# A hybrid attention block on one core: re-ordering the work around the projection tiles of its first stage

## The chip, the cores and the metric

The kernel runs on one core of a Trainium2 chip. The metric is the device time of one execution in microseconds, the median of three runs. Engines are named as in the profile: PE is TensorE (matrix products; PEld its weight loads), DVE is VectorE, ACT is ScalarE, POOL is GpSimd, SP is SyncE, which issues the DMA transfers.

## What is computed

One layer of a diffusion backbone over 2048 latent tokens and 256 context tokens of width 1024. An adaptive norm (gain and shift from `c_act @ ada_w`) is followed by one wide projection, three mixers (pooling, differential attention, grouped-query attention), each with a SiLU gate, three branch projections with sigmoid gates, an output projection and a gated residual. Cut to what matters here:

```
shift, scale, gate = split(c_act @ ada_w + ada_b, 3)
h  = rmsnorm(x, norm_g) * (1 + scale) + shift              # and the same for the context tokens
p  = split(h @ w_in)                                       # 11 pieces, 7424 columns
dq, dk, gq, gk = rope2d(rmsnorm(piece.reshape(heads, 64), g))   # per head of 64
dv, gv         = plain pieces
diff_o = rmsnorm((softmax(q1 k1) - lam * softmax(q2 k2)) @ dv)
gqa_o  = softmax(gq gk) @ gv
y   = g0 * (b0 @ w_branch[0]) + g1 * (b1 @ w_branch[1]) + g2 * (b2 @ w_branch[2])
out = x + gate * (y @ w_out)
```

## The kernel before

Numbers that need float32 accuracy are kept as two float16 parts, high and low, and a product is three passes (high x high, high x low, low x high). There are three stages.

**First stage: norm and the attention projections.** The opening makes gain and shift from `ada_w` (`ada_product`, L219), norms the first three tiles of 128 tokens (`xnorm`), turns them on PE into `tpx` (`turned_raw`, L288) and writes the two parts into `hC` (context) and `hT` (latent): `hscaled` for the first four of the eight blocks of 128 channels, `hsecond` for the last four. In `hsecond` ACT writes the high part straight from `tpx` (L323) and DVE computes the same once more into `hf` (L325) and subtracts (L328). The weights of the first kind of projection are sized and split by `w_prepare("dv")`, a generator that the opening advances step by step.

Then `project` (L532) runs over five kinds of columns in the order dv, dk, dq, gq, gkv: for each kind 18 tiles of tokens (16 for dq and gq, which leave the context out). A tile is 24 products of 128x512 (128x256 in gkv) into a buffer `qkv`, of which there are three. Between the blocks of a tile the generators in `beside` are advanced: for dv the turning and splitting of the next three token tiles (`hmake`) and the norm of the three after (`xnorm`), for the others the preparation of the next kind's weights (`w_prepare`) and a scan of all gate columns for their largest value (`scan`: a load `scan` of 512 KB a step and an ACT pass `junk`, L447, that reads it one tile later).

A tile of dk, dq, gq and gkv is followed by a chain of four steps, `qk_chain`. Step 1: ACT squares `sq` (L362), DVE sums `s` (L364, L365), POOL the power `r` (L368) and the rope tables `ab` (L374). Step 2: DVE `nt` = `qkv` * `r` (L378), POOL `rt` = `nt` * `ab` (L382), DVE `m` (L386). Step 3: DVE the add `rt<-rt,m` (L391). Step 4: PE turns `rt` into `tpq` (L396), ACT and DVE split it into `sp` (L398, L399), SP stores `sp` to `kD` or `qD` (L402). `project` advances the chains of the older tiles by one step each, the newest first, and then runs step 1 of its own tile; so three chains are under way. In dv and gkv the values go out through `vt` and `vmax` (`v_chain`, L407, L408).

In gq (`gating`) the 16 blocks of the residual gate's columns of `ada_w` are loaded (`aw`), two in a tile, and multiplied one tile later; `ada_rows` copies the two sums to `adarow`, which shares its two buffers with the gate units' `gt`.

**Gates.** 160 gate units (40 columns of 128 by four chunks of 512 tokens; `gate_unit`, 24 products, L178) are handed out as filler: `run_gates(n)` runs n units, a unit's copy `gt` is issued with the step after its 24th. `col_split` splits the next column's weights (POOL multiplies, ACT or POOL casts, POOL subtracts). One unit stands at the end of the first stage, ahead of the last steps of the chains and the turning of `adarow` (`ada_turn`, L233); two (`HEAD_UNITS - 1`) at the head of the second.

**Second stage: attention**, 256 rows of scores (L811), softmax and the products with the values (L916, L942); the gate units are spread over it by a planner that knows how much product time is left. **Third stage:** the last twelve units, branches and output.

All engines, SP too, run their instructions in the order in which the program text issues them (`manual_schedule`); what sets the order is thus the place of a call.

## Time and profile before

| what | value |
| --- | --- |
| runs (median of 3) | 2946.96 us (2945.95 to 2947.38) |
| the profiled execution, its time | 2947.69 us |
| its span, first to last instruction | 2945.9 us |
| busy in the span: PE / DVE / ACT / POOL | 2792.9 / 2268.9 / 1623.4 / 723.1 us |
| granted PE clock, mean | 0.984 |
| first stage, to the first scores | 0 to 608 us |
| attention | 608 to about 2410 us |

The rows further down are from this one execution. A timeline row gives the start in us from the span's start, the duration, the engine (SPq: an issue by SP), the line, the operation, what it writes and reads, the count of merged instructions, and in brackets how long the engine sat idle before and what ended that. A granted clock of 1.00 is 2.4 GHz, of 0.50 1.2 GHz.

### The profile page before, as it was taken

The numbers are of one execution on the slowest core, as the hardware profiler recorded it, in microseconds if no ns is written. First come the engines' busy times: TensorE is split into PE (matmuls) and PEld (weight loads), VectorE is DVE, ScalarE is ACT, GpSimd is POOL, SyncE is SP. The second block draws the span as 40 slices with busy tenths as digits, with TensorE's granted clock in tenths as the row PEclk, the third lists the DMA queues.
The fourth block names the chain that finished last, engine by engine and source line by source line (L and its number), as shares of the span: only waits on it lengthen the run. The fifth ranks groups of instructions, "written<-read, shape, count | busy, mean of one in ns | idle before, by whom it ended". The sixth has DMA issues, their size and how long they took to land. (4 is left out here: it accounts for less than half of the span.)

```text
span 2945.9 us, 41046 instructions
## 1 busy us (share of the span) xinstructions
PE 2792.9 (95%) x15031; PEld 1651.4 (56%) x15031; DVE 2268.9 (77%) x2837; ACT 1623.4 (55%) x2168; POOL 723.1 (25%) x691
## 2 busy tenths in 40 slices
PE   6999889889999999999999999999999997999999
PEld 1544434645555554555555565555555555787787
DVE  4447666578888889888889888889888856766753
ACT  3844432247666666666766777766777752322221
POOL 1036555510201121211011111111111114533421
PEclk8999999999999999999999999999999998999999
DMA  6234552269798887889899899898988967767674
GB/s 249 108 113 121 146 154 67 66 156 187 153 187 170 164 187 166 175 174 179 182 192 193 179 179 186 167 205 180 187 172 173 189 136 236 243 222 260 205 250 153
DMA packets 1134266, 516.46 MB, mean 175 GB/s; under 512 B 985040, under 2 KB 1038704, under 8 KB 1134064
## 3 DMA queue, kind: packets, MB, share of 16 engines
q1 hardware_dynamic: 1134064, 513.84, 73.8%
q8 instruction: 118, 1.93, 0.3%
q14 instruction: 84, 0.69, 0.1%
HBM read 208.24 MB, written 78.97 MB: 97 GB/s over the span
## 5 line engine op out<-in xcount | busy, mean ns | idle before, releaser
L178 PE MATMUL gate<-hT,gws 128*128 128x512 f16 x3840 | 871.4, 380 | 0.0
L178 PEld LDWEIGHTS <-gws 128*128 128x128 f16 x3840 | 374.0, 98 | 420.8 <-issue 20.5
L819 ACT ACTIVATE pt<-sa,nm,escale 128x1024 f32<-128x1024 f32 x256 | 308.3, 1204 | 453.3 <-DVE nm L816 390.2
L811 PEld LDWEIGHTS <-qt 128*128 128x128 f16 x2560 | 250.2, 98 | 353.3 <-issue 69.6
L532 PE MATMUL qkv<-wt,hT 128*128 128x512 f16 (+1 forms) x1920 | 397.6, 363 | 0.0
L815 DVE TENSOR_REDUCE nm<-sb 128x1 f32<-128x1280 f32 x256 | 379.1, 1481 | 0.4 <-PE sb L811 0.4
L814 DVE TENSOR_REDUCE nm<-sa 128x1 f32<-128x1024 f32 x256 | 311.2, 1216 | 71.4 <-PE sa L811 62.1
L820 ACT ACTIVATE pt<-sb,nm,escale 128x1280 f32<-128x1280 f32 x256 | 360.3, 1408 | 0.0
L902 DVE SCALAR_TENSOR_TENSOR lo<-pt,nm,hi 128x2304 f16<-128x2304 f32 x128 | 340.3, 2659 | 6.1 <-ACT hi L897 4.7
L811 PE MATMUL sb<-kt,qt 128*128 128x512 f16 (+1 forms) x1536 | 320.6, 345 | 18.5 <-ACT pt L820 17.5
L897 ACT ACTIVATE hi<-pt,nm 128x2304 f16<-128x2304 f32 x128 | 283.3, 2213 | 92.0 <-issue 48.8
L532 PEld LDWEIGHTS <-hT 128*128 128x128 f16 x1920 | 190.1, 100 | 177.6 <-issue 10.8
L811 PE MATMUL sa<-kt,qt 128*128 128x512 f16 x1024 | 262.7, 379 | 20.9 <-ACT pt L819 20.2
L1189 PE MATMUL br<-bt,wt 128*128 128x512 f32 x1152 | 269.1, 394 | 2.3 <-DVE wt L1044 2.3
L942 PE MATMUL av<-th,vt 128*128 128x256 f16 x2304 | 263.4, 273 | 7.9 <-DMA th<-hi 5.1
L1189 PEld LDWEIGHTS br<-bt,wt 128*128 128x128 f32 x1152 | 218.0, 189 | 52.3 <-DVE wt L1044 3.5
L942 PEld LDWEIGHTS <-vt 128*128 128x128 f16 x2304 | 225.3, 98 | 36.3 <-issue 5.1
L926 POOL TENSOR_TENSOR o<-ot 128x256 f32<-128x256 f32 x32 | 22.0, 687 | 840.4 <-ACT ot L922 840.4
L163 POOL TENSOR_SCALAR gws<-gw 128x512 f16<-128x512 f32 x74 | 76.5, 1034 | 604.8 <-PE gate L178 600.9
L916 PE MATMUL av<-th,vt 128*128 128x256 f16 x1728 | 198.9, 273 | 0.0
L1221 PE MATMUL out<-y,wt 128*128 128x512 f32 x768 | 184.1, 398 | 11.6 <-DVE wt L1044 4.9
L916 PEld LDWEIGHTS <-vt 128*128 128x128 f16 x1728 | 169.1, 98 | 19.7
(208 smaller groups left out, 3207.8 us busy)
## 6 DMA issues: line engine op xcount, KB each, us to landing
tD<-gt SPq DMA_DIRECT2D x96, 256.0 KB
wr<-in_w_br SPq DMA_DIRECT2D x32, 768.0 KB
ld<-tD SPq DMA_DIRECT2D x96, 256.0 KB
scan<-in_w_gate SPq DMA_DIRECT2D x40, 512.0 KB
gw<-in_w_gate SPq DMA_DIRECT2D x80, 256.0 KB
qt<-qD SPq DMA_DIRECT2D x256, 64.0 KB
wr<-in_w_out SPq DMA_DIRECT2D x32, 512.0 KB
sgD<-gt SPq DMA_DIRECT2D x48, 256.0 KB
```

What stands on the lines that cost most here:

```text
L178: nc.tensor.matmul(ps, lhsT=w[:, b, k, :], rhs=hT[k][:, a, c * CH:(c + 1) * CH], start=(n == 0), stop=(n == 3 * KT - 1))
L532: nc.tensor.matmul(ps[:, :width], lhsT=tokens_of(t, k, a), rhs=wt[k][:, b, :width], start=(n == 0), stop=(n == 3 * KT - 1))
L811: nc.tensor.matmul(dst, lhsT=qt[:, s, o * P:(o + 1) * P], rhs=kt[:, k0:k1], start=(s == 0), stop=(s == 1))
L814: nc.vector.tensor_reduce(out=nm[:, 0:1], in_=sa, axis=AX.X, op=ALU.max, negate=True)
L815: nc.vector.tensor_reduce(out=nm[:, 1:2], in_=sb, axis=AX.X, op=ALU.max, negate=True)
L819: nc.scalar.activation(out=pt[:, :SA], in_=sa, func=AF.Exp, scale=escale[:, m:m + 1], bias=nm[:, 0:1], accum_out=nm[:, 2:3])
L820: nc.scalar.activation(out=pt[:, SA:], in_=sb, func=AF.Exp, scale=escale[:, m:m + 1], bias=nm[:, 0:1], accum_out=nm[:, 3:4])
L897: nc.scalar.activation(out=box["hi"], in_=pt, func=AF.Copy, scale=nm[:, 3:4])
L902: nc.vector.scalar_tensor_tensor(out=lo, in0=pt, scalar=nm[:, 3:4], in1=box["hi"], op0=ALU.mult, op1=ALU.subtract)
L916: nc.tensor.matmul(ps[:, :256], lhsT=vt[:, k, v, :], rhs=pts[a][:, k, :], start=(n == 0), stop=(n == 3 * NKT - 1))
L942: nc.tensor.matmul(ps[:, :256], lhsT=vt[:, k, :, :].rearrange("p a d -> p (a d)"), rhs=pts[a][:, k, :], start=(n == 0), stop=(n == 2 * NKT ...
L1189: nc.tensor.matmul(ps, lhsT=wb[:, a, 4 * br + k, :], rhs=branch_tile(c, br, k)[:, b], start=(m == 0), stop=(m == 11))
```

## The change

- `project` runs step 1 of its own tile first and then advances the older chains (`step_chains`).
- After the last tile the remaining steps of the chains are run between gate products, 16 products before each of the three rounds (`run_steps`), where one whole unit stood ahead of all; `HEAD_UNITS` is 4, of which two stand at the head of the second stage as before. So one more unit lies ahead of the attention, and one less in it.
- In gq a tile issues the products of the blocks that were loaded two tiles before, and then its loads; `ada_rows` comes one tile later.
- `col_split` scales and casts both halves before it subtracts.
- In the opening the last part of `hsecond` takes `hf` from ACT (`turned_tokens`, two operations a block) and POOL copies it to the high part; DVE only subtracts. `w_prepare` is advanced sooner. The first tile of dv has none of the turns of the next tokens beside it; the second and third have four each instead of three.

```diff
-HEAD_UNITS = 3
+HEAD_UNITS = 4
...
     def col_split(n):
...
-            for k in range(2):
-                wr = gate_raws.pop(0)
-                hi, lo = (w[:, s, 4 * k:4 * k + 4, :].rearrange("p k d -> p (k d)") for s in range(2))
+            parts = [[gate_raws.pop(0)] + [w[:, s, 4 * k:4 * k + 4, :].rearrange("p k d -> p (k d)") for s in range(2)]
+                     for k in range(2)]
+            for wr, hi, _ in parts:
                 nc.gpsimd.tensor_scalar(out=wr, in0=wr, scalar1=gws[:, 0:1], scalar2=1.0, op0=ALU.mult, op1=ALU.mult)
...
+            for wr, hi, lo in parts:
                 nc.gpsimd.tensor_tensor(out=lo, in0=wr, in1=hi, op=ALU.subtract)
...
+    def run_steps(n):
+
+        for _ in range(n):
             if next(dense, None) is None:
                 break
+
+    def run_gates(n):
+        run_steps(24 * n)
...
-                tp = turned_raw(0, k)
-                hf = sp.tile([P, GT], F32, name="hf", tag="hf", bufs=4)
-                for (a, b, m), (_, _, d) in zip(spans(0), targets(0, k, 0)):
-                    nc.scalar.activation(out=d, in_=tp[:, a:b], func=AF.Identity, scale=gainS[:, k, m:m + 1],
-                                         bias=shiftS[:, k, m:m + 1])
-                    nc.vector.tensor_scalar(out=hf[:, a:b], in0=tp[:, a:b], scalar1=gainS[:, k, m:m + 1],
-                                            scalar2=shiftS[:, k, m:m + 1], op0=ALU.mult, op1=ALU.add)
+                hf = turned_tokens(0, k, gainS, shiftS)
+                for a, b, d in targets(0, k, 0):
+                    nc.gpsimd.tensor_scalar(out=d, in0=hf[:, a:b], scalar1=1.0, scalar2=1.0, op0=ALU.mult, op1=ALU.mult)
...
-            next(c)
-            chains.append(c)
...
+            if new:
+                next(new)
+            step_chains()
+            if new:
+                chains.append(new)
+
+        def step_chains():
             for c in chains[::-1]:
                 if next(c, "end") == "end":
                     chains.remove(c)
...
-                    at_step(making, *((2, 5, 7), (1, 3, 6), (0, 2, 4))[i])
+                    at_step(making, *(((2, 5, 7), (1, 3, 6), (0, 2, 4)) if g else ((), (1, 3, 5, 7), (0, 2, 4, 6)))[i])
...
-                if gating and u < 9:
-
-                    for m in range(2 * u, 2 * u + 2):
+                if gating and u < 10:
+
+                    for m in (2 * u - 4, 2 * u - 3):
+                        if 0 <= m:
+                            ada_product(gps[m % 2], m // 2, ada_raws.pop(0))
+                    for m in (2 * u, 2 * u + 1):
                         if m < 16:
...
-                        if m >= 2:
-                            ada_product(gps[m % 2], (m - 2) // 2, ada_raws.pop(0))
-                elif gating and u == 9:
+                elif gating and u == 10:
                     rws = ada_rows(gps)
...
-        run_gates(1)
         while chains:
-            for c in list(chains):
-                if next(c, "end") == "end":
-                    chains.remove(c)
+            run_steps(16)
+            step_chains()
         gmod = ada_turn(rws)
...
-                run_gates(HEAD_UNITS - 1)
+                run_gates(HEAD_UNITS - 2)
```

On DVE, a tile of dk (the newest tile's squares are `sq_2176` before and `sq_2221` after; `qkv_2120` is the tile before it). Before:

```order
L378 TENSOR_TENSOR nt_2157<-qkv_2058,r8_2115 128x512
L386 TENSOR_TENSOR m2_2161<-nt_2157,ab_2117 128x512
L391 TENSOR_TENSOR rt_2093<-rt_2093,m2_2095 128x512
L399 TENSOR_TENSOR sp2_2169<-tpq_2164,sp2_2169 128x512
L364 TENSOR_REDUCE s8_2178<-sq_2176 128x8
L365 TENSOR_SCALAR s8_2178<-s8_2178,wedk_1484 128x8
L489 SCALAR_TENSOR_TENSOR wt_2199<-wraw_1500,wsd_2137,wt_2199 128x512
L489 SCALAR_TENSOR_TENSOR wt_2202<-wraw_1502,wsd_2137,wt_2202 128x512
L378 TENSOR_TENSOR nt_2221<-qkv_2120,r8_2181 128x512
```

After:

```order
L489 SCALAR_TENSOR_TENSOR wt_2199<-wraw_1500,wsd_2137,wt_2199 128x512
L489 SCALAR_TENSOR_TENSOR wt_2202<-wraw_1502,wsd_2137,wt_2202 128x512
L364 TENSOR_REDUCE s8_2223<-sq_2221 128x8
L365 TENSOR_SCALAR s8_2223<-s8_2223,wedk_1484 128x8
L378 TENSOR_TENSOR nt_2231<-qkv_2120,r8_2162 128x512
L386 TENSOR_TENSOR m2_2235<-nt_2231,ab_2164 128x512
L391 TENSOR_TENSOR rt_2169<-rt_2169,m2_2171 128x512
L399 TENSOR_TENSOR sp2_2243<-tpq_2238,sp2_2243 128x512
```

The two sums moved from the end of a tile's group to its head; before, the sums `s8_2178` are followed by `nt_2221`, which needs their power `r8_2181`; after, `nt_2231` needs `r8_2162`, whose sums were written a tile earlier.

On ACT, the end of the first stage and the start of the second (`sp2` are the key copies of the last chains, `gt` a gate unit's copy, `gws` a gate column's cast). Before:

```order
L161 ACTIVATE gws_5568<-gw_4929 128x512
L161 ACTIVATE gws_5568<-gw_4931 128x512
L398 ACTIVATE sp2_5606<-tpq_5604 128x128
L398 ACTIVATE sp2_5619<-tpq_5617 128x128
L398 ACTIVATE sp2_5626<-tpq_5624 128x128
L184 ACTIVATE gt_5685<-gate_5579,ginv_121 128x512
L184 ACTIVATE gt_5713<-gate_5688,ginv_121 128x512
```

After:

```order
L161 ACTIVATE gws_5568<-gw_4929 128x512
L161 ACTIVATE gws_5568<-gw_4931 128x512
L398 ACTIVATE sp2_5605<-tpq_5603 128x128
L185 ACTIVATE gt_5617<-gate_5579,ginv_121 128x512
L398 ACTIVATE sp2_5632<-tpq_5630 128x128
L398 ACTIVATE sp2_5654<-tpq_5652 128x128
L185 ACTIVATE gt_5713<-gate_5620,ginv_121 128x512
```

The copy of the first gate unit moved ahead of the last two key copies.

On POOL, the opening (`rs` belongs to the norm, `wt` are the high parts of the weights, `hC` and `hT` the high parts of the tokens). Before:

```order
L265 TENSOR_TENSOR rs_435<-ss_376,mhalf_110 128x3
L485 TENSOR_SCALAR wt_449<-wraw_217,wsd_360 128x512
L485 TENSOR_SCALAR wt_452<-wraw_219,wsd_360 128x512
L485 TENSOR_SCALAR wt_467<-wraw_221,wsd_360 128x512
L485 TENSOR_SCALAR wt_470<-wraw_223,wsd_360 128x512
```

After:

```order
L485 TENSOR_SCALAR wt_434<-wraw_217,wsd_354 128x512
L485 TENSOR_SCALAR wt_437<-wraw_219,wsd_354 128x512
L269 TENSOR_TENSOR rs_441<-ss_376,mhalf_110 128x3
L326 TENSOR_SCALAR hC_142<-hf_448 128x256
L326 TENSOR_SCALAR hT_443<-hf_448 128x128
L485 TENSOR_SCALAR wt_455<-wraw_221,wsd_354 128x512
L485 TENSOR_SCALAR wt_458<-wraw_223,wsd_354 128x512
L326 TENSOR_SCALAR hC_142<-hf_466 128x256
L326 TENSOR_SCALAR hT_461<-hf_466 128x128
```

Two weight casts moved ahead of `rs`, and the copies of the tokens' high parts were added.

## Rows read from the trace of the kernel before

**Rows 1.** Stage windows: busy us (count) of PE, PEld, DVE, ACT, POOL; clock; DMA.

```profile
0.00:608.00 608.00, 533.88 (x2639) 265.94 (x2640) 357.25 (x686) 239.24 (x503) 252.28 (x294) 0.95 0.43 127
608.00:2410.00 1802.00, 1757.17 (x10247) 996.49 (x10246) 1593.06 (x1786) 1244.01 (x1496) 279.55 (x260) 1.00 0.87 178
```

**Rows 2.** Timeline of the opening: first products, scaling of the next tokens, their turns.

```profile
58.54 3.20 PE L532 MATMUL qkv<-wt,hC 128*128 128x512 f16 x9
...
68.14 2.07 DVE L268 TENSOR_SCALAR xt<-xt,rs 128x1024 f32<-128x1024 f32 x3
...
69.04 1.04 PE L288 MATMUL tpx<-ident,xt 128*128 128x128 f32 x2 [7.30 <-DVE xt L268]
```

**Rows 3.** Timeline of PE, dk to the start of gq.

```profile
203.82 5.34 PE L532 MATMUL qkv<-wt,hT 128*128 128x512 f16 x24
...
209.44 5.34 PE L532 MATMUL qkv<-wt,hT 128*128 128x512 f16 x24
...
312.90 0.69 PE L396 MATMUL tpq<-ident,rt 128*128 128x128 f32 x4 [4.16 <-DVE rt L391]
313.38 7.01 PE L532 MATMUL qkv<-wt,hT 128*128 128x512 f16 x24
...
411.00 3.57 PE L219 MATMUL ada<-aw,cct 128*2 128x512 f32 x4 [6.56 <-DMA aw<-in_ada_w]
...
420.82 1.88 PE L219 MATMUL ada<-aw,cct 128*2 128x512 f32 x4
```

**Rows 4.** Timeline of DVE, POOL, ACT and SP, one tile of dk.

```profile
224.54 0.68 DVE L399 TENSOR_TENSOR sp<-tpq,sp 128x512 f16<-128x512 f32 x1
...
226.16 1.64 POOL L368 TENSOR_TENSOR r<-s,mhalf 128x8 f32<-128x8 f32 x1 [2.09 <-DVE s L365]
...
226.98 0.59 ACT L362 ACTIVATE sq<-qkv 128x512 f32<-128x512 f32 x1
227.19 0.47 SPq L509 DMA_DIRECT2D scan<-in_w_gate  x1
...
227.82 0.69 DVE L378 TENSOR_TENSOR nt<-qkv,r 128x512 f32<-128x512 f32 x1 [1.75 <-POOL r L368]
...
228.62 0.69 DVE L386 TENSOR_TENSOR m<-nt,ab 128x512 f32<-128x512 f32 x1
228.69 1.75 POOL L382 TENSOR_TENSOR rt<-nt,ab 128x512 f32<-128x512 f32 x1 [0.33 <-DVE nt L378]
229.23 1.75 DVE L391 TENSOR_TENSOR rt<-rt,m 128x512 f32<-128x512 f32 x1
230.91 0.68 DVE L399 TENSOR_TENSOR sp<-tpq,sp 128x512 f16<-128x512 f32 x1
231.17 1.06 ACT L447 ACTIVATE junk<-scan 128x1024 f16<-128x1024 f32 x1 [3.60 <-DMA scan<-in_w_gate]
```

**Rows 5.** Timeline: two weight operations on DVE beside the power on POOL.

```profile
251.46 1.41 DVE L489 SCALAR_TENSOR_TENSOR wt<-wraw,wsd,wt 128x512 f16<-128x512 f32 x2
251.64 2.07 POOL L368 TENSOR_TENSOR r<-s,mhalf 128x8 f32<-128x8 f32 x1 [2.09 <-DVE s L365]
```

**Rows 6.** Timeline of PE, end of gq, gkv and the end of the stage.

```profile
497.10 5.34 PE L532 MATMUL qkv<-wt,hT 128*128 128x512 f16 x24
...
567.62 0.45 PE L396 MATMUL tpq<-ident,rt 128*128 128x128 f32 x1 [3.78 <-DVE rt L391]
...
572.98 2.78 PE L532 MATMUL qkv<-wt,hT 128*128 128x256 f16 x24
...
581.44 5.34 PE L178 MATMUL gate<-hT,gws 128*128 128x512 f16 x24
...
592.55 0.47 PE L396 MATMUL tpq<-ident,rt 128*128 128x128 f32 x1 [5.65 <-DVE rt L391]
...
595.30 12.86 PE L178 MATMUL gate<-hT,gws 128*128 128x512 f16 x48
```

**Rows 7.** Timeline of SP: the first key loads of the attention.

```profile
602.15 1.24 SPq L776 DMA_DIRECT2D kt<-kD  x2
```

More of the change, by code (lines that the diff above doesn't have):

```diff
@@ L199, in block_kernel @@
     dense = gates()
-    def run_gates(n):
-        for _ in range(24 * n):
+    def run_steps(n):
+        for _ in range(n):
             if next(dense, None) is None:
                 break
+    def run_gates(n):
+        run_steps(24 * n)
     with tc.tile_pool(name="p1", bufs=1) as sp, tc.tile_pool(name="p1s", bufs=1, space=PSUM) as pp:
@@ L536, in project @@
                     next(s, None)
+            e = weps[kind]
+            new = None
+            if kind == "dk":
+                new = qk_chain(ps, 8, GAIN["dk"], t, e, lambda i: (kD[i], t))
+            elif kind == "dq":
+                new = qk_chain(ps, 8, GAIN["dq"], t, e, lambda i: (qD[i], t - NCT))
+            elif kind == "gq":
+                new = qk_chain(ps, 8, GAIN["gq"], t, e, lambda i: (qD[4 + i], t - NCT))
+            elif kind == "gkv":
+                v_chain(ps, 128, 128, gvD, 1, t)
+                new = qk_chain(ps, 2, GAIN["gk"], t, e, lambda i: (kD[4], t))
+            else:
+                v_chain(ps, 0, 512, vD, 0, t)
+            if new:
[4 more added lines that the diff above has]
+        def step_chains():
             for c in chains[::-1]:
@@ L539, in project @@
                     chains.remove(c)
-            e = weps[kind]
-            if kind == "dk":
-                c = qk_chain(ps, 8, GAIN["dk"], t, e, lambda i: (kD[i], t))
-            elif kind == "dq":
-                c = qk_chain(ps, 8, GAIN["dq"], t, e, lambda i: (qD[i], t - NCT))
-            elif kind == "gq":
-                c = qk_chain(ps, 8, GAIN["gq"], t, e, lambda i: (qD[4 + i], t - NCT))
-            elif kind == "gkv":
-                v_chain(ps, 128, 128, gvD, 1, t)
-                c = qk_chain(ps, 2, GAIN["gk"], t, e, lambda i: (kD[4], t))
-            else:
-                v_chain(ps, 0, 512, vD, 0, t)
-                return
-            next(c)
-            chains.append(c)
         xs, hf0, chains, beside = {}, [], [], {}
@@ L646, in block_kernel @@
                     next(wp)
-            if n == 14:
-                next(wp)
-            if n == 15:
+            for _ in range({13: 2, 14: 1, 15: 2}.get(n, 0)):
                 next(wp)
         rws = ada_rows(aps[1])
-        next(wp)
-        for _ in range(2):
-            next(wp)
         norming = xnorm(1)
@@ L662, in block_kernel @@
             next(hs)
+        next(wp)
         next(norming)
```

## The prediction

> **What bounds the kernel now.** I read the stage windows first. From 608 to 2410 us TensorE is busy 1757.17 of 1802 us, 97.5%; from 0 to 608 it is busy 533.88 of 608, and at a granted clock of 0.95 instead of 1.00 [rows 1]. So the attention stage is at TensorE's pace, and the first stage, which nearly all of the edits touch, has 74 us in which TensorE does nothing, and some more that it loses at the lower clock level. The chain of waits of that stage, and then the timeline, say where they lie.
>
> An unhindered tile of dk, dq or gq takes 5.62 us (203.82 to 209.44) [rows 3]. But TensorE gets there only while it has slack. In the dk tiles VectorE goes round in 6.37 us (sp2 at 224.54, again at 230.91) [rows 4]. The reader is to see one idle gap in that ring: `nt` waits 1.75 us for `r`, which POOL starts only after VectorE has written the two sums, since the sums of the newest tile stand last in VectorE's order and `nt` of the same tile comes next. The second thing to see is `rt` on POOL (1.75) beside the add `rt<-rt,m` on VectorE (1.75), against 0.69 for `m`, which has the same shape [rows 4]: the two lie on each other. When the slack is gone TensorE's turns wait for the add.
>
> **The change, part by part** (against the profiled execution, 2947.69 us; its span is 2945.9, and the median of the runs, 2946.96, is 0.7 us below it).
>
> *Sums first (B: dk, dq, start of gq).* Now VectorE does the sums of tile t, then `nt`, `m` of t-1, the add of t-2, `sp` of t-3. Nothing is added; `r` has a whole tile to arrive, so the 1.75 us wait goes. VectorE's work for a tile is 0.94 (the two sums, between 225.22 and 226.16), 0.69, 0.69, the add, and 0.68 [rows 4]. With the add at 0.69, as `m` has it, that is 3.7 us; at 1.75 it is 4.75. Both are below 5.62. What is late next is a ring through the scan of the gate columns: `sp` to the next scan issue on SP (224.54 to 227.19, 2.65, the stores lie between), issue to the `junk` that reads it (227.19 to 231.17, 3.98), `junk` 1.06, `sq` 0.59, which now stands behind `junk` and ahead of all of the chain, then 0.94 + 0.69 + 0.69 + the add until `sp` again [rows 4]. That is 11.3 us with the short add and 12.35 with the long one, for two tiles: 5.65 or 6.2 us a tile. In the new order the add runs while POOL does `r` and `ab`, not `rt`. The nearest row for such an overlap is a pair of `wt` operations beside `r`: they take 1.41 for two, and it is `r` that stretches, from 1.64 to 2.07 [rows 4, 5]. So I take the short add and 5.7 us a tile.
> From 203.82 to the end of gq's second tile (411.00 less its 6.56 us of waiting, 404.4) are 31 tiles: 200.6 us [rows 3]. At 5.7 they take 176.7: 23.9 less. One event I leave in: where the next weights' loads come in a burst, TensorE waits 4.16 us for the add and then runs a tile of 5.34 us in 7.01 [rows 3]; the burst is still there, and half of it, 3 us, may stay. **B = 21**, with ends 8 (6.2 us a tile) and 26 (5.62).
>
> *Gate columns two tiles ahead (C).* The first products of the gate rows wait 6.56 us for their load, and four of them then take 3.57 where four take 1.88 later [rows 3]: 8.2 us. The loads keep their place; the products come one tile, 5.6 us, later. So some 1 us of waiting is left. **C = 7**, ends 5 and 8.2. That ada products stand beside tiles u = 2 to 9 instead of 1 to 8 costs nothing, there are 16 in either.
>
> *The end of gq, and gkv (D).* From 497.10 to the first gate product at 581.44 are 84.3 us [rows 6]. It holds two tiles of 5.62, eighteen gkv tiles of 2.78, and beside three of these still the wide turns, 0.3 each (5.62 less 5.34): 62.2 at full pace, 22.1 less. gkv has the same ring in small, and the same wait goes. Kept: some 2 us at the entry, where three wide chains (3.7 each) meet tiles of 3 us, and 1.5 of the 3.78 us [rows 6] behind the split of the first gate column on POOL; both halves now go to ScalarE before POOL subtracts. **D = 18.5**, ends 11 and 22.
>
> *Last stages between gate products (F, G).* From 581.44 to the end of 48 gate products at 608.16 (595.30 + 12.86) TensorE takes 26.7 us for 72 products, 5.65 of it in one wait for an add, and 48 products cost 12.86 rather than 10.7 since the clock had dropped [rows 6]. The new order has 96 products there, 21.4, and three turns (0.47 at most) and the turned gate rows, all of it some 2.0 of the 2.75 between 592.55 and 595.30: 23.4. A wait is added: the copy `gt` of the first gate unit uses the buffer of the gate rows, so ScalarE waits in it until these are turned; queued behind it are the last two key copies, their stores, the value scales and the loads of the attention. Today the first keys are issued at 602.15, 6.85 us after the turned rows' end [rows 6, 7]; with `gt` and two copies ahead some 8.5. The 48 products cover 10.7, and the keys must land by then: 0 to 3 us of waiting, I take 0.5. **F = 3**, ends 0 and 5. The 24 products more are 24 fewer in the attention, at 97.5% on TensorE: 5.3 at most, **G = 4**, ends 0 and 5.3.
>
> *The opening (A).* The first tile holds three sets of turns of the next tokens, and TensorE waits 7.30 us for them, until VectorE has scaled the tokens at 68.14; nine products before it took 3.20 us, 0.36 each, where warm ones take 0.22 [rows 2, 3]. The turns leave that tile (four in each of the next two instead of three), VectorE loses eight operations on the way to the scaling, POOL gains eight, and the weights' scale is made some us sooner. No row shows POOL's copies; they stand behind weight casts on POOL, which VectorE waits for anyway. Upper end: the 7.30 and 24 products back at the full rate, 10. Lower: ScalarE, with eight turns' copies and three squares now in two tiles, gives 4 back: 3. **A = 8**, near the wait, which has no other owner.
>
> Nothing else moves: columns of the gate weights keep their POOL time, only re-sorted. Sum: 8 + 21 + 7 + 18.5 + 3 + 4 = 61.5; 2947.7 - 61.5 = 2886, and with the 0.7 us to the median **2885 us**.
>
> **Rivals.** *1. VectorE's two-operand operations lose to POOL.* In today's ring `m` starts 0.07 us before `rt`, and `rt` is long; the add starts after `rt` and is long [rows 4]: who comes first keeps the other off. If `r` (1.64) and the two `ab` keep `m` and the add off in the same way, the add costs 1.75 or more, the ring 6.2 us: B = 8, and gkv pays 0.4 in each of 15 tiles: D = 12. Sum 42: 2905. Against it: the pair of `wt`, two operands from the same memory, beside `r`, was not slowed [rows 5].
> The Trainium skill has this as a rule (SBUF — State Buffer, "Who interferes with whom"): VectorE with two SBUF inputs and a GpSimd operation that reads SBUF exclude each other for the whole instruction, the first one winning. `rt` against the add agrees with it; `wt` beside `r` does not, at least not for the whole of `r`. By the rule this rival would be the forecast.
> *2. Everything at TensorE's pace*: all upper ends, 76 us: 2870. It needs the burst and the first loads to vanish too.
> *3. The scan still sets the pace.* If its loads take a microsecond or two longer at the faster pace, a tile stays at 6.4, B is 2 and A 4: 2915 to 2930. For it: SP issues scan and stores in one order; against: ScalarE waits 3.60 us for the scan today without TensorE feeling it.
> *4. Slower.* In the new order POOL's `r`, `ab` and `rt` all fall beside `m` and the add. If both must sit out what POOL has queued, `m` waits for `r` and `ab` (about 2.3) and the add for `rt`: the two-tile ring is 14 us, 7.0 a tile, B = -16 and gkv some 9 over. That alone is the break-even with A, C, F and G. From 7.0 us a tile on it is slower; with TensorE's clock dropping in each of those gaps (7.01 for 5.34 [rows 3]) it costs some 10 us more: 2960. That needs every arbitration lost, where the rows show one lost and one won.
> That the edit is not what it says can be left out: the order on each engine shows it.
>
> **How the numbers follow.** Forecast (2872 to 2895): 0.58. Rival 1 (2895 to 2914): 0.25. Rival 2 (2866 to 2872): 0.08. Rival 3: 0.06. Rival 4: 0.03. A range of 2869 to 2914 leaves out rivals 3, 4 and half of 2. The measurement can tell 0.2% (6 us) from no change. Faster: 0.96; same 0.015, for rival 4 at its break-even; slower 0.025.
>
> **What would show it.** VectorE's `nt` no longer waits for `r`, and its add beside `r` takes about 0.7, not 1.75 (1.75: rival 1). TensorE's turns in dk and dq have no wait over 0.3 us apart from the burst; gkv tiles go every 2.7 to 2.9 us. The first ada product waits under 2 us. The first turn of the second token group comes near 65, not 69. The first scores begin some 55 us sooner than today. I am wrong if ScalarE's `sq` is found waiting behind `junk` tile after tile, or if the first scores wait for keys for more than 3 us.

## The result, and the profile after

The kernel after takes 2910.44 us (median of 4 runs, 2908.53 to 2912.96) against 2947.17 beside it: ratio 0.9878, interval 0.9866 to 0.989. It is faster by 36.7 us, at the slow end of the range (2869 to 2914), where 61.5 us were forecast. The direction and the mechanism of the largest term came out, but only F had its size: A was too low, and B, C, D and G were too high.

To see where, I take the same marks in both traces and ask how much sooner each comes. "Sooner" is the lead over the kernel before; what the lead grows from one mark to the next is what the stretch between them gave, and it stands under "measured" beside the term of the prediction for that stretch (us).

| mark | before | after | sooner | term | forecast | measured |
|---|---|---|---|---|---|---|
| dv, fourth tile | 88.34 | 77.05 | 11.30 | A opening | 8 | 11.3 |
| gq, second tile | 397.90 | 370.40 | 27.50 | B sums first | 21 | 16.2 |
| gq, eleventh tile | 473.97 | 444.88 | 29.09 | C gate rows | 7 | 1.6 |
| first gate product | 581.44 | 540.43 | 41.01 | D end of gq, gkv | 18.5 | 11.9 |
| first scores | 608.00 | 563.70 | 44.30 | F last stages | 3 | 3.3 |
| first branch product | 2468.36 | 2431.40 | 36.96 | G attention | 4 | -7.3 |
| end | 2945.88 | 2908.19 | 37.7 | | | 0.7 |

The miss, 23.8 us, is G (11.3), D (6.6), C (5.4) and B (4.8), less the 3.3 that A brought more and 1.0 in F and behind the last mark. The windows of the kernel after show both sides (columns as in [rows 1]): the first stage is 44 us shorter and still has 34 us in which TensorE is idle, and the attention, with 24 products fewer in it, is longer than before, where the same stretch took 1860.36.

```profile
0.00:563.70 563.70, 529.75 (x2663) 269.68 (x2664) 313.92 (x678) 239.87 (x504) 233.31 (x304) 0.96 0.47 138
563.70:2431.40 1867.70, 1797.84 (x10412) 1014.80 (x10413) 1621.91 (x1826) 1256.55 (x1516) 299.14 (x278) 0.99 0.87 179
```

**An unhindered tile of dk after** (timeline; it answers to [rows 4]): `nt` follows the newest sums with no wait, the add stands beside `r` and takes 0.69, and VectorE is done with the tile in 3 us. From here to the end of dk the tiles go at 5.62 us, but for two with the products of the next weights' scale in them (5.72 and 6.03) and the last, 6.40. `sq` stands behind a `junk` that waits for the scan, 4.05 us, and TensorE does not feel it.

```profile
205.01 0.68 DVE L378 TENSOR_TENSOR nt<-qkv,r 128x512 f32<-128x512 f32 x1
205.18 1.64 POOL L368 TENSOR_TENSOR r<-s,mhalf 128x8 f32<-128x8 f32 x1 [2.02 <-DVE s L365]
205.80 0.69 DVE L386 TENSOR_TENSOR m<-nt,ab 128x512 f32<-128x512 f32 x1
206.41 0.69 DVE L391 TENSOR_TENSOR rt<-rt,m 128x512 f32<-128x512 f32 x1
207.51 1.26 POOL L382 TENSOR_TENSOR rt<-nt,ab 128x512 f32<-128x512 f32 x1
209.26 1.06 ACT L447 ACTIVATE junk<-scan 128x1024 f16<-128x1024 f32 x1 [4.05 <-DMA scan<-in_w_gate]
210.32 0.58 ACT L362 ACTIVATE sq<-qkv 128x512 f32<-128x512 f32 x1
```

**Where the next weights are loaded**, TensorE now stops for longer than before. In dq (first group below) SP issues eight weight loads and behind them the scan's; ScalarE's `junk` waits 6.30 us for it, `sq` comes behind, and TensorE waits 4.92. Two tiles take 11.14 and 7.65, the second in part at the lower clock level (granted clock 0.69 from 288.3 to 296.4); [rows 3] had a wait of 4.16. In gq the same happens (second group): the gate columns' product does not wait any more, where it waited 6.56 us in [rows 3], but the turn ahead of it does.

```profile
273.04 3.79 SPq L460 DMA_DIRECT2D wraw<-in_w_qkv  x8
276.88 0.43 SPq L509 DMA_DIRECT2D scan<-in_w_gate  x1
283.58 1.06 ACT L447 ACTIVATE junk<-scan 128x1024 f16<-128x1024 f32 x1 [6.30 <-DMA scan<-in_w_gate]
288.34 1.08 PE L396 MATMUL tpq<-ident,rt 128*128 128x128 f32 x4 [4.92 <-DVE rt L391]
...
372.23 4.04 SPq L460 DMA_DIRECT2D wraw<-in_w_qkv  x8
381.74 1.06 ACT L447 ACTIVATE junk<-scan 128x1024 f16<-128x1024 f32 x1 [6.66 <-DMA scan<-in_w_gate]
386.50 1.08 PE L396 MATMUL tpq<-ident,rt 128*128 128x128 f32 x4 [4.71 <-DVE rt L391]
387.51 3.57 PE L223 MATMUL ada<-aw,cct 128*2 128x512 f32 x4
```

**gkv**: its steady tiles take 2.73 us (3.42 before). At the entry the add meets POOL's `rt` and takes 1.75, TensorE waits 3.04 and then has the lower clock for a tile (granted clock 0.54 from 488.9 to 495.2). Such a tile, at the lower clock level after a wait, is called cold from here on. Behind the first column's split ScalarE's copy waits for POOL, the next tile's `vt` and `sq` stand behind it, and TensorE waits 2.38, with a cold tile again (4.45 for 24 products that take 2.78 otherwise).

```profile
486.44 1.75 POOL L382 TENSOR_TENSOR rt<-nt,ab 128x512 f32<-128x512 f32 x1
486.98 1.75 DVE L391 TENSOR_TENSOR rt<-rt,m 128x512 f32<-128x512 f32 x1
488.88 1.09 PE L396 MATMUL tpq<-ident,rt 128*128 128x128 f32 x4 [3.04 <-DVE rt L391]
...
521.11 1.30 ACT L161 ACTIVATE gws<-gw 128x512 f16<-128x512 f32 x2 [2.87 <-POOL gw L159]
522.32 0.26 ACT L407 ACTIVATE vt<-qkv 128x128 f32<-128x128 f32 x1
524.96 0.33 PE L396 MATMUL tpq<-ident,rt 128*128 128x128 f32 x1 [2.38 <-DVE rt L391]
525.12 4.45 PE L532 MATMUL qkv<-wt,hT 128*128 128x256 f16 x24
```

**The first scores** (here `sa`) wait 0.78 us behind the gate products; the forecast had 0.5 for the keys.

```profile
552.40 10.52 PE L179 MATMUL gate<-hT,gws 128*128 128x512 f16 x48 [0.53 <-ACT gt L185]
563.70 1.02 PE L812 MATMUL sa<-kt,qt 128*128 128x512 f16 x4 [0.78 <-POOL gws L163]
```

**In the attention** one row of scores takes 13.19 us where the same row took 6.52 before. That is 6.7 us. The stage is 7.3 us longer, and 24 products fewer should have made it some 5 us shorter (0.22 us each), so nearly as much again is lost in other rows, such as the one at 670.91 (8.45, 6.52 before) and the one at 2242.88 (9.96, 8.70 before). In the long row it goes like this: POOL splits a gate column; SP stands in the load that refills the column's buffer until the subtraction is over; the transposed loads of the parts (`th`) stand behind that load on SP, which has hardly a pause from there to the one issued at 1465.36; for that one TensorE waits, three rows after the one in which the hold began, and then runs at the lower clock level (0.22 us a product, where 36 take 4.09 below).

```profile
1442.92 4.58 POOL L165 TENSOR_TENSOR gws<-gw,gws 128x512 f16<-128x512 f32 x2
1444.11 3.76 SPq L150 DMA_DIRECT2D gw<-in_w_gate  x2
1449.28 2.83 SPq L849 DMA_TRANSPOSE th<-hi  x1
1465.36 4.32 SPq L849 DMA_TRANSPOSE th<-hi  x1
1471.74 4.00 PE L943 MATMUL av<-th,vt 128*128 128x256 f16 x18 [3.34 <-DMA th<-hi]
```

Ahead of the same row of the kernel before, the load came when the subtraction was over, and the products did not wait:

```profile
1497.02 1.16 POOL L164 TENSOR_TENSOR gws<-gw,gws 128x512 f16<-128x512 f32 x1
1499.45 0.87 SPq L150 DMA_DIRECT2D gw<-in_w_gate  x2
1510.73 4.09 PE L942 MATMUL av<-th,vt 128*128 128x256 f16 x36
```

### The profile page after: what moved, and what is told of

The parts are those of the page before. It is cut to its first block, busy times and chain, and to the rows that moved or that the text cites. A ratio compares the mean times of both kernels' runs of the same rounds, so it can differ in the third digit from the quotient of the medians.

```text
span 2908.2 us, 41087 instructions
## 1 busy us (share of the span) xinstructions
PE 2787.0 (96%) x15031; PEld 1653.7 (57%) x15031; DVE 2222.6 (76%) x2829; ACT 1623.7 (56%) x2168; POOL 699.2 (24%) x699
## 5 line engine op out<-in xcount | busy, mean ns | idle before, releaser
L532 PEld LDWEIGHTS <-hT 128*128 128x128 f16 x1920 | 189.7, 99 | 176.8 <-issue 11.3
L163 POOL TENSOR_SCALAR gws<-gw 128x512 f16<-128x512 f32 x74 | 68.2, 922 | 597.7 <-PE gate L179 593.8
```

The lines of the kernel that those rows point to most:

```text
L532: nc.tensor.matmul(ps[:, :width], lhsT=tokens_of(t, k, a), rhs=wt[k][:, b, :width], start=(n == 0), stop=(n == 3 * KT - 1))
```

## The experiments

Times are medians; the kernels of one group shared the runs of the kernel before (2947.67, 2946.87 and 2947.70 us in the three groups). "First scores" and "attention" (first scores to first branch product) come from the profiled execution of each kernel. The code is cut; `...` marks what is left out.

### The sums first alone

On the kernel before, only this (the loop over the older chains becomes `step_chains`, and is called behind the new tile's first step):

```diff
+            if new:
+                next(new)
+            step_chains()
+            if new:
+                chains.append(new)
+
+        def step_chains():
             for c in chains[::-1]:
                 if next(c, "end") == "end":
                     chains.remove(c)
...
-            next(c)
-            chains.append(c)
```

> The kernel before with one part of the change alone: a tile's sums and its first step are issued ahead of the older tiles' steps (opening, gate columns, last stages as before). Theory 1 (the sum's terms B and D were too large, since the stalls where the next weights and the first gate columns are loaded, and the entry into gkv, do not go away with the order): tiles of dk and dq at 5.62 us but one tile of dq near 11 us; gained by the end of gq's second tile 14 to 18 us, over gq's end and gkv 9 to 13, attention as before (first scores to the first branch product 1860 us): about 2921 us (2915 to 2927). Theory 2 (the terms were right, B = 21 and D = 18.5, and what the sum missed was lost elsewhere by the other edits): 2947 - 39.5 = about 2908. Theory 3 (the add is slowed beside POOL, 6.2 us a tile): tiles at 6.2 us, about 2927 to 2930, with the add at 1.75 us in the rows.

Measured: 2930.12 us, ratio 0.9944 (0.9927 to 0.996): 17.5 us, a smaller gain than any theory but the third had. Theory 3 falls all the same, since the tiles of dk go at 5.62 and not at 6.2, although the total is about the one that it gave. What theory 1 has right are the stalls: a dq tile takes 12.27, the first tile with gate rows 17.04, and the split's tile 6.90. It missed one: with the products one tile behind their loads, gq has further tiles of 10.00, 9.00 and 10.86, and the lead over the kernel before falls from 13.6 us to 5.2 across them. At the first scores it is 20.9; the attention takes 1863.0.

### Gate rows one tile behind their loads

```diff
-                if gating and u < 10:
+                if gating and u < 9:
...
-                    for m in (2 * u - 4, 2 * u - 3):
+                    for m in (2 * u - 2, 2 * u - 1):
...
-                elif gating and u == 10:
+                elif gating and u == 9:
```

> The kernel after, with the products of the gate rows one tile behind their loads, as in the kernel before, in place of two. Theory 1 (the distance is worth more than the 1.6 us by which the lead grows across these tiles, since in the kernel with the sums first alone, where the products stand one tile behind, the lead fell by 8.4 us across the same tiles, with tiles of 10.00, 9.00 and 10.86 us where 7.53 is the pace): several gq tiles of 9 to 11 us, first scores 8 to 12 us later than 563.7, total 2918 to 2922. Theory 2 (the burst of loads costs the same either way and the distance gives the 1.6 to 3.5 us read from the lead): 2911 to 2914. Theory 3 (the term C = 7 of the sum): 2916 to 2918.

Measured: 2920.25 us (0.9912, 0.9897 to 0.9927), 9.8 us over the kernel after; first scores at 576.34. Theory 1 holds. The products wait for their loads at every second tile:

```profile
387.28 3.57 PE L223 MATMUL ada<-aw,cct 128*2 128x512 f32 x4 [8.03 <-DMA aw<-in_ada_w]
407.63 1.88 PE L223 MATMUL ada<-aw,cct 128*2 128x512 f32 x4 [2.82 <-DMA aw<-in_ada_w]
442.47 2.65 PE L223 MATMUL ada<-aw,cct 128*2 128x512 f32 x4 [2.79 <-DMA aw<-in_ada_w]
```

Across these tiles the lead falls from 24.4 to 14.4 us. So the distance is worth about 10 us, and the 1.6 of the table is not its worth but what is left of it after the stall in gq: with the sums first and the old distance, 8 to 10 us are lost there.

### Weight loads spread

```diff
-            if not final:
+            if n == 0:
                 for k in range(KT):
                     w_load(QKV_ORDER[n + 1], k)
...
+                if n and not final and u < 4:
+                    for k in (2 * u, 2 * u + 1):
+                        w_load(QKV_ORDER[n + 1], k)
                 project(kind, width, wt, t)
```

> The kernel after, with the eight loads of the next weights (for dk, dq and gq) issued two at a time ahead of the first four tiles, in place of eight ahead of the first. Theory 1 (the two long stalls after the change, one dq tile of 11.14 us and the gq tile of 14.57 us, are the scan's load that stands behind eight weight loads, with ScalarE's squares behind the scan): both go, the dq tiles stay at 5.62 us and the first gq tile with gate columns takes 7.5 to 8.5; first scores at 547 to 552 us instead of 563.7, total 2895 to 2899. Theory 2 (it is the bytes of that stretch, so that spreading only spreads the delay): first scores within 4 us of 563.7 and several tiles near 7 us; 2907 to 2911.

Measured: 2902.91 us (0.9848, 0.9833 to 0.9863), between the two theories; first scores at 558.81, though its opening was 2 us late. The gq tile falls from 14.57 to 8.48. In dq the stall is only drawn out: tiles of 6.31, 7.95 and 7.30 in place of 11.14 and 7.65. Two weight loads ahead of each scan are enough to make TensorE wait:

```profile
289.97 1.06 ACT L447 ACTIVATE junk<-scan 128x1024 f16<-128x1024 f32 x1 [5.22 <-DMA scan<-in_w_gate]
294.72 0.63 PE L396 MATMUL tpq<-ident,rt 128*128 128x128 f32 x4 [2.14 <-DVE rt L391]
```

### A third buffer for the scan

The burst stays, and the scan is loaded a tile earlier. The room comes from two other tiles, which lose a buffer each: `ab` has two instead of three, and `vt` of the value tiles one instead of two (these lines are left out):

```diff
...
-            for i in range(41):
+            for i in range(42):
                 if i < 40:
-                    t = sp.tile([P, D], F32, name="scan", tag="scan", bufs=2)
+                    t = sp.tile([P, D], F32, name="scan", tag="scan", bufs=3)
...
-                if i:
-                    size_of(gmx[:, i - 1:i], tiles[i - 1])
+                if i > 1:
+                    size_of(gmx[:, i - 2:i - 1], tiles[i - 2])
```

> The kernel after, with three buffers for the scan of the gate columns in place of two: each load is issued one tile earlier than it is read (room for it from one buffer less of vt in the value tiles and of ab). Theory 1 (the two-tile ring through the scan has no slack, so each burst of weight loads stops ScalarE's squares and TensorE for as long as it lasts; 2 x 256 KB ahead of each scan already cost a stall of 7.95 us and a cold tile of 7.30 in the spread version): the dq tile of 11.14 us and its cold successor go to 5.62 to 6.5, the gq tile of 14.57 to 7.5 to 9; first scores at 548 to 552 instead of 563.7; total 2894 to 2899. Theory 2 (TensorE waits for VectorE's add for another reason there, such as the weights' sizes on ScalarE behind their own loads): the stalls stay above 9 and 12 us; 2906 to 2912.

Measured: 2892.97 us (0.9816, 0.9799 to 0.9832), 17.5 us under the kernel after; first scores at 545.72. Theory 1 holds: the dq tiles take 5.62 (5.73 and 6.03 with the scale's products in them), and the gq tile 8.45. By gq's eleventh tile, with the opening set apart, 15.8 us are gained; the rest is in gkv, where this execution has one cold tile less. A scan still lands late behind the eight weight loads, but it is read a tile later, and the turn that waited 4.92 us waits no more:

```profile
273.02 3.79 SPq L460 DMA_DIRECT2D wraw<-in_w_qkv  x8
276.85 0.44 SPq L509 DMA_DIRECT2D scan<-in_w_gate  x1
283.52 0.60 PE L396 MATMUL tpq<-ident,rt 128*128 128x128 f32 x4
284.14 1.06 ACT L447 ACTIVATE junk<-scan 128x1024 f16<-128x1024 f32 x1 [4.34 <-DMA scan<-in_w_gate]
289.14 0.60 PE L396 MATMUL tpq<-ident,rt 128*128 128x128 f32 x4
```

### Three gate units ahead, as before

```diff
-HEAD_UNITS = 4
+HEAD_UNITS = 3
...
-            run_steps(16)
+            run_steps(8)
...
-                run_gates(HEAD_UNITS - 2)
+                run_gates(HEAD_UNITS - 1)
```

> The kernel after, with three gate units ahead of the scores as in the kernel before, in place of four: 8 gate products in each round of the last stages in place of 16, and 48 ahead of the second row. Theory 1 (the attention is 7 us longer after the change, 1867.7 us from the first scores to the first branch product against 1860.4, because the gate columns' splits and loads fall on other rows, above all behind the row where TensorE waits 3.3 us for a transposed load): attention back to 1859 to 1863 though it has 24 products more, first scores 2 to 5 us sooner than 563.7; total 2898 to 2905. Theory 2 (the loss comes with the earlier start, whatever the number of units): attention 1870 to 1874 with the 24 products, total 2909 to 2914.

Measured: 2901.26 us (0.9849, 0.9834 to 0.9864); attention 1862.49 with 24 products more in it, first scores at 560.97. Theory 1 holds: the row of 13.19 us takes 6.52 again. The row's stall is there in all six other kernels that have the attention of the kernel after unchanged (the list below the next heading), wherever between 545 and 577 us their first scores come. It goes with how the columns fall on the rows, not with the time of the start. The re-sorted `col_split` is in this kernel too, so it does not make the stall by itself; whether four units with the old split would have it is not shown.

### The next gate column loaded one unit later

```diff
             gate_split.append(w)
-            col_load(n + 2)
...
             gate_now[0] = gate_split.pop(0)
+        if u % NCH == 1:
+            col_load(u // NCH + 3)
...
                         col_split(0)
+                        col_load(2)
```

> The kernel after, with the load of the next gate column issued on SP one gate unit later than the split that frees its buffers, in place of right behind it. Theory 1 (in the attention SP waits in that load for POOL's last subtraction, 3.7 us between 1444.1 and 1447.9, and the transposed loads stand behind it, so TensorE waits for them some rows later): no wait of TensorE for a transposed load over 2 us, attention 1858 to 1863 us instead of 1867.7; total 2900 to 2906. Theory 2 (the transposed loads are late because the DMA engines are full, 0.91 busy in that stretch): waits of about the same sum, 1865 to 1870; total within 4 us of 2910.

Measured: 2898.07 us (0.9832, 0.9818 to 0.9847), 12.4 us under the kernel after, though its first scores come 2.5 us later; attention 1852.38, more gained than theory 1 had it. The stage is shorter with the DMA engines as full as in the kernel after (0.88 against 0.87), so theory 2 falls. SP now issues the transposed load before POOL has begun to subtract, 7 us sooner, and the one for which TensorE waited 5.4 us sooner; the products of that row do not wait. TensorE's waits for transposed loads fall from 16.7 us in all to 1.7 (7.7 in the kernel before). Besides the row of 13.19 us, which takes 6.52, three more rows gain most: 9.96, 9.47 and 8.45 us become 6.74 each.

```profile
566.16:2418.54 1852.38, 1794.30 (x10412) 1014.23 (x10412) 1620.75 (x1825) 1255.58 (x1516) 297.29 (x277) 1.00 0.88 180
```

```profile
1442.01 2.74 SPq L851 DMA_TRANSPOSE th<-hi  x1
1442.70 4.58 POOL L165 TENSOR_TENSOR gws<-gw,gws 128x512 f16<-128x512 f32 x2
1456.40 0.89 SPq L150 DMA_DIRECT2D gw<-in_w_gate  x2
1459.99 3.88 SPq L851 DMA_TRANSPOSE th<-hi  x1
1468.01 4.09 PE L945 MATMUL av<-th,vt 128*128 128x256 f16 x36
```

The attention of all kernels (us), the kernels with three units ahead first: before 1860.35, sums first alone 1863.0, three units 1862.5; four units: after 1867.7, third scan buffer 1869.1, weights spread 1868.1, gate rows near 1869.3, turns back 1865.9, split in steps 1866.7, early weights 1869.1; with the later loads 1852.4.

### The later load on the kernel before

The same edit on the kernel before:

```diff
-            col_load(n + 2)
...
+        if u % NCH == 1:
+            col_load(u // NCH + 3)
...
+                        col_load(2)
```

> The kernel before, with the load of the next gate column issued one gate unit later than the split that frees its buffers, and nothing else. With that edit the kernel after went from 1867.7 to 1852.4 us between the first scores and the first branch product. Theory 1 (the hold of SP costs the kernel before less, as its columns fall on better rows, and without it both take the same time but for the 24 products, 5.1 us): 1856 to 1859 us there instead of 1860.4, total 2942 to 2946; the term G was right but for the hold. Theory 2 (the hold costs the kernel before as much): 1847 to 1850, total 2933 to 2937. Theory 3 (no hold in the kernel before at all): 1860, total 2946 to 2948.

Measured: 2943.80 us (0.9989, 0.998 to 0.9998), attention 1858.42. Theory 1 holds. Without the hold of SP the kernel before takes 1858.4 and the kernel after 1852.4; the 6.0 us between them are about what the 24 products take (5.3). Kernels with one and the same attention differ by up to 3.4 us in the list above, so no more is read from that, and the 1.9 us by which the attention got shorter here is not clear of it; the 3.1 us of the total are clear of noise. SP's waits in that load during the attention are, of the kernel before and of the kernel after (us in total, times, longest):

```profile
SPq L150 <- POOL gws L164: 43.6, 22, 4.4
```

```profile
SPq L150 <- POOL gws L165: 47.5, 24, 3.6
```

The hold is nearly as large in both. Without it the attention gets 1.9 us shorter in the one and 15.3 in the other: what it costs depends on the rows on which it falls. The difference, 13.4 us, covers the 11.3 by which G missed.

### The turns back in the first tile

```diff
-                    at_step(making, *(((2, 5, 7), (1, 3, 6), (0, 2, 4)) if g else ((), (1, 3, 5, 7), (0, 2, 4, 6)))[i])
+                    at_step(making, *((2, 5, 7), (1, 3, 6), (0, 2, 4))[i])
```

> The kernel after, with the turns of the second token group in all three first tiles (three, three, two), as in the kernel before, in place of the last two; the earlier weight steps and POOL's copies in the opening stay. Theory 1 (the 11.3 us of the opening are the wait of 7.3 us for the turns and the clock behind it): a wait of 5 to 8 us in the first tile is back, first scores 8 to 10 us later than 563.7. Theory 2 (the earlier scaling of the tokens and the shorter way of VectorE make most of it): the wait is under 3 us, first scores 0 to 4 us later.

Measured once: 2910.97 us. The wait is back, 5.20 us and cold products behind it, and the fourth tile comes 6.2 us later; the other edits of the opening thus bring 5.1 of the 11.3, and which of them is not told apart. The rows are the first tile here and then in the kernel after:

```profile
56.17 3.22 PE L532 MATMUL qkv<-wt,hC 128*128 128x512 f16 x9
64.59 1.05 PE L292 MATMUL tpx<-ident,xt 128*128 128x128 f32 x2 [5.20 <-DVE xt L272]
```

```profile
55.87 9.28 PE L532 MATMUL qkv<-wt,hC 128*128 128x512 f16 x30
64.98 0.38 PE L292 MATMUL tpx<-ident,xt 128*128 128x128 f32 x2
```

At gq's eleventh tile it is 7.8 us behind the kernel after, at the first scores only 2.7, and in the total nothing. So the wait is theory 1's, and the first scores are theory 2's. In gkv this execution did not have the cold tiles behind the waits (2.78 where the kernel after had 5.20, and again 2.78 for 4.45), and the attention was 1.9 us shorter. One run does not say whether that repeats.

### The first column's split in steps, and the gkv weights earlier

The first spreads the split over the gkv tiles 8 to 14 (POOL scaling with its copy, again, a subtraction, again; the generator `col_split_steps` is left out); the second takes four steps of the weights more in gq:

```diff
-                    if u == 10:
-                        col_split(0)
+                    if u == 8:
+                        splitting = col_split_steps(0)
+                    if u in (8, 9, 11, 13, 14):
+                        next(splitting, None)
...
```

```diff
                         at_step(coming, 3)
+                    if gating and u in (10, 11, 12, 13):
+                        at_step(coming, 5)
```

> The kernel after, with the split of the first gate column in five steps over the gkv tiles 8 to 14 (one POOL scaling with its ScalarE copy, then the other, then one subtraction, then the other) in place of all of it behind tile 10. Theory 1 (TensorE's wait of 2.38 us there and the slow tile behind it come from the 5.1 us that POOL spends in one piece ahead of the next tile's r): no wait over 0.6 us in those tiles, first scores 2.5 to 4.3 us sooner than 563.7 for an equal opening. Theory 2 (a subtraction of 1.15 us beside 1.8 us of a tile's own POOL work is more than the 2.73 us of a tile has room for): two waits of 0.3 to 1 us, 1 to 2 us sooner.

> The kernel after, with four more steps of the gkv weights' preparation in gq's tiles 10 to 13, so that the last casts and VectorE's small operations on the scale are done some tiles before gkv begins. Theory 1 (VectorE's 1.84 us of casts and 1.55 us of small operations, which stand in the last gq tile and the first gkv tile, are why the entry into gkv loses 3.97 us in its second tile and 1.2 in its first): the first two gkv tiles take 2.8 to 4.5 us each instead of 3.95 and 6.70, first scores 3 to 6 us sooner for an equal opening. Theory 2 (it is the wide chains of gq's last tiles, with the add of 1.75 us behind POOL's rt): the second tile stays at 5.5 to 6.7, under 1.5 us sooner.

Measured once each: 2908.05 and 2908.82 us. In the first, neither theory has the cause. TensorE waits twice, 1.39 and 1.54 us, behind the two scalings and not behind the subtractions: ScalarE's copy stands at the head of its queue until POOL has scaled, and the next tile's `vt` and `sq` stand behind it. The two tiles lose 3.4 us where the kernel after lost 4.3.

```profile
515.05 0.63 ACT L159 ACTIVATE gws<-gw 128x512 f16<-128x512 f32 x1 [2.88 <-POOL gw L158]
515.58 0.26 ACT L420 ACTIVATE vt<-qkv 128x128 f32<-128x128 f32 x1
517.90 0.33 PE L409 MATMUL tpq<-ident,rt 128*128 128x128 f32 x1 [1.39 <-DVE rt L404]
```

In the second, the second gkv tile takes 4.77 in place of 6.70, and the wait is 1.53 in place of 3.04: half of that tile's loss was the casts and the scale's small operations on VectorE, as theory 1 has it; the other half stays, with the add of 1.75 us, as theory 2 has it. The first tile keeps its 3.95.

### Together

The third scan buffer with the later column loads:

> The kernel after with two edits that were run apart, the third scan buffer (2893.0) and the later gate column loads (2898.1). Theory 1 (they lie in different stages and add): 2910.4 - 17.5 - 12.4 = 2880.5 (2876 to 2884), attention near 1852 us, first scores near 547. Theory 2 (how the attention's columns fall changes with the start, so that its gain is in part luck): attention 1857 to 1866, 2885 to 2892.

Measured: 2878.88 us (0.9768, 0.9755 to 0.9781), first scores at 549.59, attention 1853.26. Theory 1 holds: the two add.

And with the split in steps and the early weights besides:

> The kernel with the third scan buffer and the later gate column loads, and also the split of the first gate column in five steps and the earlier gkv weights. Expected from the theories of the four: 2880.5 less 2.6 for the split and 3 to 5 for the entry, 2872 to 2877. If the last two edits do nothing, 2880; if POOL's subtractions or the added steps disturb the gkv and gq tiles, above 2882.

Measured: 2877.23 us (0.9759, 0.9746 to 0.9773), at the upper edge of what was expected and not told apart from the one without them. By its median it is the fastest of the kernels, some 33 us under the kernel after and 70 under the kernel before. Its first scores come at 546.62, and its attention takes 1852.28.

## Why the prediction was right or wrong

**B, the mechanism: right; the size: not.** `nt`'s wait went and the tiles reached TensorE's pace, a little better than the 5.7 us that I took. The step that failed is "half of it, 3 us, may stay", for the burst. The stall there grew to 7.6 us (11.14 and 7.65 less two of 5.62). I had the ring through the scan at 11.3 us for two tiles, which is right, and then used it as a rate. With TensorE at 11.24 for two tiles that ring has no slack, and so a late load passes whole into TensorE's time. That is rival 3 in small: the scan does not set the pace, it sets the stalls. The third buffer shows it. The term of 3 us for the burst thus measured 7.6, and that is nearly all of the 4.8 us by which B missed.

**C: the wrong owner.** The step that failed is "some 1 us of waiting is left". The product's own wait did go, but the same burst delays the scan, and the turn ahead of the product waits 4.71 us. It was also mis-sized the other way: at the new pace the old distance would have cost some 10 us more than I knew of, as the kernel with it shows. The two roughly cancel.

**D: two kept terms mis-sized.** For the entry into gkv I kept 2 us; its first three tiles lost 7.9 (3.95, 6.70 and 5.47 less 2.73 each), of which I had counted 0.9 as wide turns; half of the wait there comes from casts and small operations that I had not looked for in that tile. For the column's split I kept 1.5; it took 4.3, and its cause is not POOL's subtraction, which the re-sorting moves, but ScalarE's copy that waits at the head of its queue. Some of both is the lower clock behind the wait. The steady tiles were right (2.73, forecast 2.7 to 2.9).

**F: right** (3.3, forecast 3): behind the 48 products the first scores wait 0.78 us, where I took 0.5.

**G: right as work, wrong as time.** The two kernels without the hold are 6.0 us apart there, where I had 5.3 at most for the 24 products. The step that failed is that I counted them as a pure loss of work in a stage at 97.5%. One unit more ahead of the stage also shifts the gate columns against the rows of scores, and in the kernel after one column's load holds SP's queue just where the transposed loads are wanted. I listed SP among the queues for the last stages, and did not ask what the shift does to it further on. The shift could be seen in the order; which row it would hit, and for how much, I could not have read from the trace of before, but that the load waits for POOL 22 times with transposed loads behind it could be.

**A: too low.** The wait is not all of it: putting the turns back costs 6.2 us, and the other edits of the opening, the earlier weights and the shorter way to the scaling among them, brought 5.1 more. The step that failed is "near the wait, which has no other owner": I had counted nothing for them above the wait.

**The rivals.** Rival 1 fell where the forecast placed it. Over all tiles after, the add's durations are (minimum, median, maximum):

```profile
L391 DVE TENSOR_TENSOR rt<-rt,m x64: 278/685/1751, 195.2 to 548.1; 128x512 f32<-128x512 f32 x48, 128x128 f32<-128x128 f32 x16
```

The wide add takes 0.69 us 47 times of 48, in 46 of them beside `r` and `ab`; it is 1.75 once, at the entry into gkv, where it meets `rt`. The Trainium skill (SBUF — State Buffer, "Who interferes with whom") says that a VectorE instruction with two SBUF inputs contends with a GpSimd instruction that reads SBUF, and calls the contention an exclusive lock. This case agrees for `rt` with the add and disagrees for `r` and `ab`, both of which read SBUF, beside the add and beside `m` (0.69 at most). The total came within rival 1's bounds (2895 to 2914), and for none of its reasons. My own forecast (2872 to 2895) missed it; that the stated range holds the result is therefore in part luck, since the range was that wide for rival 1's sake. Rival 3's bounds do not follow from its terms: B = 2 and A = 4 with the other terms kept make 38.5 us, 2908 and not 2915 to 2930. Rival 4's price was never paid: neither `m` nor the add waits for POOL in dk, dq or gq.

**The signs that I named.** Held: `nt` without a wait, the add at 0.7, the turn of the second group at 64.98, gkv at 2.73 once its entry is over, the first gate-row product without a wait of its own, the keys. Not held: the first scores 55 us sooner (44.3), and no wait over 0.3 us outside the burst (0.59 ahead of the first dq tile). And one of the two signs of being wrong came: in 27 of the 50 wide tiles of the kernel after, `sq` starts right behind a `junk` that has waited over 1 us for its scan (1 of 50 before, 2 of 50 with the third buffer). In most of them TensorE does not feel it. But it shows the ring without slack in every second tile, and a burst on top of it makes the stalls in B and C.

## What to carry to other kernels

When an edit brings an engine to its pace, look at the next ring not by its mean but by its slack: a ring that just keeps up passes every late transfer on, and one buffer more, with one less for two other tiles, was worth 17.5 us here. A load that waits for a buffer holds all that its queue has behind it, so issue it when the buffer is already free; that cost nothing to write and gave 12 us. And whatever changes the amount of work ahead of a long, regular stage also shifts its phase against the queues: bound that with the waits that are already there, even when they cost nothing today.

## What was not expected of the hardware

- The same wait does not always cost the clock. At the entry into gkv TensorE waited 3.04 or 3.05 us in two kernels with the same order there, and the next tile took 5.20 us in one and 2.78 in the other (5.21, 4.45 and 3.89 in further ones).
- POOL's `rt` and VectorE's add, 1.26 and 0.69 us apart from each other, take 1.75 both where they meet. In these rows `m` is still under way when `rt` starts, and `rt` gets longer by about what is left of `m` (in the kernel before 1.47 with 0.34 us left, 1.75 with 0.62); the add then ends 0.54 us behind `rt`. So the first seems to hold the next off. But `r` of 1.64 us leaves the same add, and `m`, at 0.69.
- Kernels with the same opening began their second tile between 63.6 and 65.6 us; differences of 2 us at the first scores in one profile are therefore not read as effects.
